# Hybrid encoder layer: pieces multiplied in halves of 256 columns, tokens and sums 16 bytes up in their tiles

## The chip, the cores and the metric

The kernel runs on one core of one Trainium2 chip. The metric is device time in microseconds (us) of one execution, as the median of several runs of the same program. One further execution is taken with the hardware profiler; the profile and the trace below are of that one.

## The reference

One layer of an encoder on 256 tokens of width 4096, all in float32: a layer norm, one wide input projection, a gated short convolution and a windowed attention side by side, one output projection, a residual and a second layer norm.

```python
h = layer_norm(x, emb_ln_g, emb_ln_b)                 # (256, 4096)
p = h @ w_in                                          # (4096, 13312): c_b c_c c_h c_z | q k v | z
y_conv = c_b * centred_short_conv(c_c * c_h, conv_w) * silu(c_z)
y_attn = banded_window_attention(a_q, a_k, a_v, sink) * silu(a_z)
y = concatenate([y_conv, y_attn]) @ w_out             # (4096, 4096)
out = layer_norm(2 ** 0.25 * h + y, ln_g, ln_b)
```

Nearly all arithmetic is in the two projections.

## The kernel before

**Numbers in two halves.** TensorE multiplies in a reduced float32 (F32R). To keep the accuracy, each operand is split in a high half, which is the rounded number, and a low half, which is what the rounding left. A product is then three matmuls: high by high, high by low, low by high. ScalarE writes the high half of the weights (`split_hi`, L203) and VectorE the low half (`split_lo`, L207).

**Operands.** The tokens are the stationary operand: tile `xT` (L228) holds, turned, 32 blocks of 128 rows, each with 256 tokens high and 256 tokens low. The weights stream through as the moving operand. They come from HBM over SyncE's queue in units that a fixed list of steps names (`steps`, L116), into raw tiles (`load`, L139; `loads`, L159), and the halves go to the tiles `whi` and `wlo`, three of each, 8192 bytes a partition.

**Two kinds of steps.** A *piece* is four blocks of 128 rows by 512 columns of weights. `mm` (L237) multiplies it for the input projection and `mm_out` (L904) for the output projection: per block and per half of the tokens three matmuls of 512 columns into a PSUM bank. A *pair* is a Strassen-like step: two blocks of rows by two halves of 256 columns, seven products instead of eight. VectorE adds up sums of the weights' blocks (`sums`, L169), sums of the tokens lie in the tiles `SC`, `SC2` and, in the output projection, `SCy` (`x_sums`, L638; `y_sums`, L997), and `mm_pair` (L257) does 7 × 3 matmuls of 256 columns into the accumulators `acc` and `pacc`. Most column chunks of the input projection have 18 blocks in pieces and 14 in pairs; five chunks of the output projection have four pairs. The last two chunks of the output projection are 256 columns wide, so their matmuls in `mm_out` have 256 columns already.

**Placement.** Tiles of a pool lie one behind the other in each partition. `xT` is 65,536 bytes and the weights' pool follows it at once, so pieces have tokens and weights that both start at multiples of 128 bytes. For pairs the split writes the seven blocks 16 elements, that is 64 bytes, lower in the tile (`SHIFT`, L51; `dst`, L192), and `split_lo` then cuts `wh` and `wl` to these seven blocks, so that `mm_pair` reads block `w - 1`. `SC`, `SC2` and `SCy` start at multiples of 128 bytes too.

**Order.** Every engine takes its instructions in the order in which the program lists them. In the loop over the input steps (L802) step j comes as: the matmuls of j, the high half of step j + 3, work due at j (ends of chunks, attention, convolution), new loads, the weight sums of j + 4, the low half of j + 3. The loop over the output chunks (L1007) has the same order. So the halves run three steps ahead of the matmuls, and there are three tiles for each half.

Of the kernel before, what the change touches and what calls it, by code (L numbers as in the profile page):

```python
# [8 lines left out]
F32 = mybir.dt.float32  # L9
F32R = mybir.dt.float32r  # L10
AF = mybir.ActivationFunctionType
ALU = mybir.AluOpType
AX = mybir.AxisListType

P = 128
D = 4096
S = 256
KT = D // P
# [14 lines left out]
W = 512  # L33
PK = PIECE // W
# [6 lines left out]
HW = W // 2  # L41
HT = S // 2
NP = 7
# [4 lines left out]
OP = 4  # L48
OUT_ORDERS = ["s" * 8] * 2 + ["sSsSsSsSss"] * 5 + ["", ""]
N_W = 3  # L50
SHIFT = 16  # L51


def units(ci):
# [32 lines left out]
def npairs(ci):  # L87
    return PAIRS[ci] if ci < OUT else OUT_ORDERS[ci - OUT].count("S")
# [11 lines left out]
def encoder_kernel(ctx: ExitStack, tc: tile.TileContext, x, emb_g, emb_b, wi, ws, conv_w, sink, wo, ln_g, ln_b, out):  # L100
    nc = tc.nc
    PSUM = bass.MemoryType.PSUM

    const = ctx.enter_context(tc.tile_pool(name="const", bufs=1))
    wpool = ctx.enter_context(tc.tile_pool(name="wpool", bufs=3))
    small = ctx.enter_context(tc.tile_pool(name="small", bufs=4))
# [13 lines left out]
    is_pair = lambda j: steps[j][0] in ("pair", "opair")  # L120

    raw, wh, wl = {}, {}, {}
    psc = pw = pc = R = None
# [62 lines left out]
    def part(j, t):  # L186

        if len(raw[j].shape) == 3:
            return t if len(t.shape) == 3 else t.rearrange("p (i n) -> p i n", i=2)
        return t[:, HW:] if is_pair(j) else t[:, 0:4 * HW] if steps[j][0] == "half" else t  # L190

    def dst(j, t):  # L192

        return t[:, HW - SHIFT:8 * HW - SHIFT] if is_pair(j) and len(raw[j].shape) == 2 else part(j, t)

    def half_tile(j, name):
        if j < len(steps) - 1:
            return wpool.tile([P, PIECE], F32R, name=name)
        (_, k), bs = w_bufs(j)
        user[bs[k]] = j  # L200
        return bs[k][0].tile([P, PIECE], F32R, name=bs[k][1], bufs=1)

    def split_hi(j):  # L203
        wh[j] = half_tile(j, "whi")
        nc.scalar.activation(dst(j, wh[j]), part(j, raw[j]), AF.Copy)  # L205

    def split_lo(j):  # L207
        wl[j] = half_tile(j, "wlo")
        nc.vector.tensor_tensor(dst(j, wl[j]), part(j, raw[j]), dst(j, wh[j]).bitcast(F32), op=ALU.subtract)  # L209
        if is_pair(j):  # L210
            c0 = HW if len(raw[j].shape) == 3 else HW - SHIFT
            wh[j], wl[j] = wh[j][:, c0:c0 + 7 * HW], wl[j][:, c0:c0 + 7 * HW]
        raw.pop(j)

    def split(j):
        if j < len(steps):
            split_hi(j)
            split_lo(j)
# [6 lines left out]
    cw = const.tile([P, CONV_T, 3], F32, name="cw")  # L225
    sk = const.tile([P, HEADS], F32, name="sk")

    xT = const.tile([P, KT, 2 * S], F32R, name="xT")  # L228
    musd = small.tile([P, 2, 4], F32, name="musd", bufs=1)
    eps_t = small.tile([P, 1], F32, name="eps_t", bufs=1)  # L230
    nc.vector.memset(eps_t, LN_EPS)
    small.tile([P, 40], F32, name="gap", bufs=1)


    acc = {}
# [1 line left out]
    def mm(j):  # L237
        _, ci, q = steps[j]
        hi, lo = wh.pop(j), wl.pop(j)
        first = j == 0 or steps[j - 1][1] != ci  # L240
        last = j == N_IN - 1 or steps[j + 1][1] != ci
        pk, k0 = (2, 2 * q) if steps[j][0] == "half" else (PK, q * PK)
        for k in range(pk):
            kt = k0 + k
            for i in range(2):
                if first and k == 0:
                    acc[ci, i] = ps_acc.tile([P, W], F32, name="acc")
                a = acc[ci, i]
                xh, xl = xT[:, kt, i * P:(i + 1) * P], xT[:, kt, S + i * P:S + (i + 1) * P]
                hk, lk = hi[:, k * W:(k + 1) * W], lo[:, k * W:(k + 1) * W]  # L250
                nc.tensor.matmul(a, xh, hk, start=(first and k == 0), stop=False)  # L251
                nc.tensor.matmul(a, xh, lk, start=False, stop=False)  # L252
                nc.tensor.matmul(a, xl, hk, start=False, stop=(last and k == PK - 1))  # L253

    pacc, SC = {}, None

    def mm_pair(j):  # L257


        _, ci, p = steps[j]  # L260
        hi, lo = (t.pop(j).rearrange("p (b w) -> p b w", w=HW) for t in (wh, wl))
        last = p == npairs(ci) - 1
        if p == 0:
            for k in range(2):
                pacc[ci, k] = ps_p.tile([P, 2, HW], F32, name="pacc")
        a, b = 2 * p, 2 * p + 1
        x = lambda kt, i: (xT[:, kt, i * HT:(i + 1) * HT], xT[:, kt, (2 + i) * HT:(3 + i) * HT])
        sc = lambda n: (SC[p][:, 0, n, :], SC[p][:, 1, n, :])
        p0, p1, c0, c1 = pacc[ci, 0], pacc[ci, 1], acc[ci, 0], acc[ci, 1]
        for (ah, al), w, o, opens, closes in (  # L270
                (x(a, 0), 2, p0[:, 0, :], True, False), (x(b, 0), 3, c0[:, 0:HW], False, False),
                (sc(2), 1, c0[:, HW:W], False, False), (x(b, 1), 7, c1[:, 0:HW], False, False),
                (sc(0), 5, p1[:, 1, :], True, False), (x(a, 1) if ci < OUT else sc(3), 6, p0[:, 1, :], False, True),
                (sc(1), 4, p1[:, 0, :], False, True)):
            nc.tensor.matmul(o, ah, hi[:, w - 1, :], start=(opens and p == 0), stop=False)  # L275
            nc.tensor.matmul(o, ah, lo[:, w - 1, :], start=False, stop=False)  # L276
            nc.tensor.matmul(o, al, hi[:, w - 1, :], start=False, stop=(closes and last))  # L277


    def small_chain(i, dst):  # L280
# [10 lines left out]
    with tc.tile_pool(name="pro", bufs=1) as pro:  # L291
# [15 lines left out]
        first = [wpool.tile([P, PIECE], F32, name=f"first{j}", tag="whi") for j in range(2)]  # L307
# [103 lines left out]
        transp2(2, (1,))  # L411
        turned1(1, 0, t1[0])
        split_hi(2)
        first_mm(0, 1)
        transp2(3, (1,))
        turned1(1, 1, t1[1])
        first_mm(1, 1)
        turned2(2)
        split_lo(2)
        load(5)  # L420
        x_split(2)
# [3 lines left out]
        load(6)  # L425
        transp2(4)
        mm(2)
        turned2(4)
        x_split(4)
        split(4)  # L430
        load(7)
        transp2(5)
        mm(3)
        turned2(5)
        x_split(5)
        split(5)
        load(8)
        transp2(6)
        mm(4)
        turned2(6)  # L440
        x_split(6)
# [17 lines left out]

    ph, phs = ExitStack(), ExitStack()  # L460
    psc = ctx.enter_context(tc.tile_pool(name="psc", bufs=1))
    sc_tiles = [psc.tile([P, n, 2, 3, HT], F32R, name=name) for n, name in ((NP - 2, "SC"), (2, "SC2"))]
    SC = [sc_tiles[p // (NP - 2)][:, p % (NP - 2), :, :, :] for p in range(NP)]
    pw = phs.enter_context(tc.tile_pool(name="pw", bufs=1))
    extra.append((pw, "w6"))
# [336 lines left out]
    for j in range(n_pro, N_IN):  # L802
        kind, ci, q = steps[j]
        if j == z0 + 4:
            extra.clear()
        if j == z0 + 12:
            extra.insert(0, (pw, "w6"))
        mm_pair(j) if kind == "pair" else mm(j)
        split_hi(j + 3)
        for fn, a in later.pop(j, []):  # L810
            fn(*a)
        if kind == "pair" and q == PAIRS[ci] - 1:
            pair_copy(ci)
# [12 lines left out]
        split_lo(j + 3)  # L826
# [77 lines left out]
    def mm_out(j, n, halves, k0=0, k1=None):  # L904
        c0, w, pk, j0 = chunks[n]
        ci, q = steps[j][1:]
        hi, lo = wh[j], wl[j]
        for k in range(k0, k1 or pk):
            s = q * pk + k
            first, last = j == j0 and k == 0, s == KT - 1  # L910
            for i in halves:
                if first:
                    acc[ci, i] = ps_acc.tile([P, 512], F32, name="acc")[:, 0:w]
                o = acc[ci, i]
                yh, yl = xT[:, s, i * P:(i + 1) * P], xT[:, s, S + i * P:S + (i + 1) * P]
                hk, lk = hi[:, k * w:(k + 1) * w], lo[:, k * w:(k + 1) * w]
                nc.tensor.matmul(o, yh, hk, start=first, stop=False)  # L917
                nc.tensor.matmul(o, yh, lk, start=False, stop=False)  # L918
                nc.tensor.matmul(o, yl, hk, start=False, stop=last)  # L919

    def plus_res(n):

# [84 lines left out]
    for n, (c0, w, pk, j0) in enumerate(chunks):  # L1007
        us = out_units(n)
        np_ = sum(u[0] == "opair" for u in us)
        for t, (kind, _, q) in enumerate(us):  # L1010
            j = j0 + t
            if kind == "opair":
                mm_pair(j)
            else:
                mm_out(j, n, (0,) if n == ncs - 1 else (0, 1))
# [114 lines left out]
```

## Time and profile before

| | |
|---|---|
| median of 3 runs | 1528.76 us (1528.3 to 1529.1) |
| profiled execution, whole | 1529.49 us |
| profiled execution, span from first to last instruction | 1527.8 us |
| TensorE clock granted | 1.000 on the mean |
| DMA | 315.65 MB, 207 GB/s on the mean |
| ScalarE, GpSimd busy | 51%, 0% |

Engines in the profile: PE is TensorE's matmul, PEld its weight load (it overlaps PE), DVE is VectorE, ACT ScalarE, POOL GpSimd, SP SyncE. A group's row names line, engine, operation, tiles (out<-in) and shapes, then the count, the busy time in us and the mean duration of one in ns, then the idle time before it and what ended that. A matmul's duration contains the drain of the pipe, which overlaps with the next matmul; the distance between two starts is read from the timeline, whose rows give start in us, duration in us, engine, line, operation, tiles, shape and count.

### The profile page before, as it was taken

The numbers are of one execution on the slowest core, as the hardware profiler recorded it, in microseconds if no ns is written. First come the engines' busy times: TensorE is split into PE (matmuls) and PEld (weight loads), VectorE is DVE, ScalarE is ACT, GpSimd is POOL, SyncE is SP. The second block draws the span as 40 slices with busy tenths as digits, with TensorE's granted clock in tenths as the row PEclk, the third lists the DMA queues.
The fourth block names the chain that finished last, engine by engine and source line by source line (L and its number), as shares of the span: only waits on it lengthen the run. The fifth ranks groups of instructions, "written<-read, shape, count | busy, mean of one in ns | idle before, by whom it ended". The sixth has DMA issues, their size and how long they took to land.

```text
span 1527.8 us, 21818 instructions
## 1 busy us (share of the span) xinstructions
PE 1511.7 (99%) x8879; PEld 1330.0 (87%) x8879; DVE 1329.4 (87%) x1555; ACT 780.7 (51%) x669; POOL 1.3 (0%) x7
## 2 busy tenths in 40 slices
PE   7999999999999999999999999999999999999998
PEld 4888989898988989989889888888988888888897
DVE  7769899999899898998898899989898688888876
ACT  5545546657565655545555455544556444444431
POOL 0000000000000000000000000000000000000000
PEclk9999999999999999999999999999999999999999
DMA  7555654555654556656555655556557655666573
GB/s 289 208 179 193 207 207 162 205 179 196 210 182 171 185 185 205 230 183 234 199 190 202 215 189 202 207 175 234 198 203 291 257 200 215 257 213 214 215 248 131
DMA packets 71716, 315.65 MB, mean 207 GB/s; under 512 B 8544, under 2 KB 12608, under 8 KB 50880
## 3 DMA queue, kind: packets, MB, share of 16 engines
q1 hardware_dynamic: 70608, 312.43, 58.4%
q10 hardware_dynamic: 1008, 1.84, 0.3%
q8 instruction: 69, 1.13, 0.3%
q14 instruction: 31, 0.25, 0.0%
HBM read 305.23 MB, written 8.91 MB: 206 GB/s over the span
## 4 chain that ended last, share of the span: by engine, by line
PE 83%; DVE 12%; ACT 2%; DMA 1%; issue 1%; SPq 0%; ACTq 0%; DVEq 0%
PE acc L252 13%; PE acc L253 13%; PE acc L251 13%; DVE wlo L209 7%; PE acc L918 6%; PE acc L919 6%; PE acc L917 6%; PE pacc L275 4%; PE pacc L277 4%; PE pacc L276 4%; PE acc L275 3%; PE acc L277 3%; PE acc L276 3%; ACT whi L205 2%; DVE w L182 1%
## 5 line engine op out<-in xcount | busy, mean ns | idle before, releaser
L205 ACT ACTIVATE whi<-w 128x2048 fp32r<-128x2048 f32 (+1 forms) x354 | 621.5, 1756 | 621.8 <-DVE w L184 218.2
L209 DVE TENSOR_TENSOR wlo<-w,whi 128x2048 fp32r<-128x2048 f32 (+1 forms) x354 | 736.4, 2083 | 123.7 <-ACT whi L205 123.5
L251 PE MATMUL acc<-whi,xT 128*128 128x512 f32 x988 | 387.4, 392 | 0.0
L252 PE MATMUL acc<-wlo,xT 128*128 128x512 f32 x988 | 386.0, 391 | 0.3
L253 PE MATMUL acc<-whi,xT 128*128 128x512 f32 x988 | 385.1, 390 | 0.0
L252 PEld LDWEIGHTS acc<-wlo,xT 128*128 128x128 f32 x988 | 185.5, 188 | 39.4 <-DVE wlo L209 3.6
L253 PEld LDWEIGHTS acc<-whi,xT 128*128 128x128 f32 x988 | 185.4, 188 | 38.1
L251 PEld LDWEIGHTS acc<-whi,xT 128*128 128x128 f32 x988 | 185.5, 188 | 35.0
L918 PE MATMUL acc<-wlo,xT 128*128 128x512 f32 (+1 forms) x480 | 175.1, 365 | 1.0 <-DVE wlo L209 1.0
L917 PE MATMUL acc<-whi,xT 128*128 128x512 f32 (+1 forms) x480 | 175.1, 365 | 0.0
L919 PE MATMUL acc<-whi,xT 128*128 128x512 f32 (+1 forms) x480 | 174.9, 364 | 0.0
L182 DVE TENSOR_TENSOR w<-w 128x512 f32<-128x512 f32 x179 | 122.3, 683 | 10.2 <-DMA w<-in_ws 10.2
L918 PEld LDWEIGHTS acc<-wlo,xT 128*128 128x128 f32 x480 | 90.6, 189 | 15.3 <-DVE wlo L209 1.7
L275 PE MATMUL acc<-whi,xT 128*128 128x256 f32 x370 | 103.7, 280 | 0.0
L276 PE MATMUL acc<-wlo,xT 128*128 128x256 f32 x370 | 103.7, 280 | 0.0
L277 PE MATMUL acc<-whi,xT 128*128 128x256 f32 x370 | 103.7, 280 | 0.0
L919 PEld LDWEIGHTS acc<-whi,xT 128*128 128x128 f32 x480 | 90.5, 189 | 14.3
L917 PEld LDWEIGHTS acc<-whi,xT 128*128 128x128 f32 x480 | 90.6, 189 | 13.9 <-issue 0.4
L275 PE MATMUL pacc<-whi,xT 128*128 128x256 f32 x350 | 99.8, 285 | 0.0
L276 PE MATMUL pacc<-wlo,xT 128*128 128x256 f32 x350 | 98.3, 281 | 0.0
L277 PE MATMUL pacc<-whi,xT 128*128 128x256 f32 x350 | 98.1, 280 | 0.0
L277 PE MATMUL pacc<-whi,SC 128*128 128x256 f32 x330 | 92.5, 280 | 0.0
(230 smaller groups left out, 2059.4 us busy)
## 6 DMA issues: line engine op xcount, KB each, us to landing
w<-in_wi SPq DMA_DIRECT2D x112, 1024.0 KB
w<-in_ws SPq DMA_DIRECT2D x202, 512.0 KB
w<-in_wo SPq DMA_DIRECT2D x41, 1024.0 KB
R<-in_wo SPq DMA_DIRECT2D x13, 1024.0 KB
x<-in_x SPq DMA_DIRECT2D x7, 512.0 KB
yl<-yd SPq DMA_DIRECT2D x7, 512.0 KB
xc<-in_x SPq DMA_DIRECT2D x14, 256.0 KB
R<-in_ws SPq DMA_DIRECT2D x6, 512.0 KB
```

The source lines that it names most:

```text
L182: nc.vector.tensor_tensor(s01, b22, b12.to_broadcast([P, 2, HW]), op=ALU.add)
L205: nc.scalar.activation(dst(j, wh[j]), part(j, raw[j]), AF.Copy)
L209: nc.vector.tensor_tensor(dst(j, wl[j]), part(j, raw[j]), dst(j, wh[j]).bitcast(F32), op=ALU.subtract)
L251: nc.tensor.matmul(a, xh, hk, start=(first and k == 0), stop=False)
L252: nc.tensor.matmul(a, xh, lk, start=False, stop=False)
L253: nc.tensor.matmul(a, xl, hk, start=False, stop=(last and k == PK - 1))
L275: nc.tensor.matmul(o, ah, hi[:, w - 1, :], start=(opens and p == 0), stop=False)
L276: nc.tensor.matmul(o, ah, lo[:, w - 1, :], start=False, stop=False)
L277: nc.tensor.matmul(o, al, hi[:, w - 1, :], start=False, stop=(closes and last))
L917: nc.tensor.matmul(o, yh, hk, start=first, stop=False)
L918: nc.tensor.matmul(o, yh, lk, start=False, stop=False)
L919: nc.tensor.matmul(o, yl, hk, start=False, stop=last)
```

## The change

Three edits. In `mm` and `mm_out` a matmul of 512 columns becomes two of 256, the three products of the left half first, then those of the right half; stationary operands are named again for each half. The shift of the pairs' weights by 64 bytes goes (`SHIFT`, `dst` and the cut in `split_lo`), so that all weights' blocks start at multiples of 1024 bytes in their tiles. And a new function `shifted` gives tiles that are 32 bytes longer than their content, which begins 16 bytes in: `xT`, `SC` and `SC2` come from it, `SCy` does not. `musd`, `eps_t` and a filler go from the pool `small` to `const`, which, with the 32 bytes of `xT`, moves the weights' pool up by 128 bytes; a second filler makes `small` 128 bytes smaller, so that the pools behind it begin where they began. With that, the tokens and sums start 16 bytes past a multiple of 128 and the weights on one, that is 112 bytes past the tokens modulo 128.

```diff
-SHIFT = 16
+OFF = 4
...
-    def dst(j, t):
-
-        return t[:, HW - SHIFT:8 * HW - SHIFT] if is_pair(j) and len(raw[j].shape) == 2 else part(j, t)
...
-        nc.scalar.activation(dst(j, wh[j]), part(j, raw[j]), AF.Copy)
+        nc.scalar.activation(part(j, wh[j]), part(j, raw[j]), AF.Copy)
...
-        nc.vector.tensor_tensor(dst(j, wl[j]), part(j, raw[j]), dst(j, wh[j]).bitcast(F32), op=ALU.subtract)
-        if is_pair(j):
-            c0 = HW if len(raw[j].shape) == 3 else HW - SHIFT
-            wh[j], wl[j] = wh[j][:, c0:c0 + 7 * HW], wl[j][:, c0:c0 + 7 * HW]
+        nc.vector.tensor_tensor(part(j, wl[j]), part(j, raw[j]), part(j, wh[j]).bitcast(F32), op=ALU.subtract)
...
-    xT = const.tile([P, KT, 2 * S], F32R, name="xT")
-    musd = small.tile([P, 2, 4], F32, name="musd", bufs=1)
-    eps_t = small.tile([P, 1], F32, name="eps_t", bufs=1)
+    def shifted(pool, shape, name, **kw):
+
+        n = math.prod(shape)
+        t = pool.tile([P, n + 2 * OFF], F32R, name=name, **kw)[:, OFF:OFF + n]
+        names = "abcd"[:len(shape)]
+        return t.rearrange(f"p ({' '.join(names)}) -> p {' '.join(names)}", **dict(zip(names[1:], shape[1:])))
+
+    xT = shifted(const, (KT, 2 * S), "xT")
+    musd = const.tile([P, 2, 4], F32, name="musd")
+    eps_t = const.tile([P, 1], F32, name="eps_t")
     nc.vector.memset(eps_t, LN_EPS)
-    small.tile([P, 40], F32, name="gap", bufs=1)
+    const.tile([P, 8], F32, name="gap")
+    small.tile([P, 24], F32, name="gap2", bufs=1)
...
-                hk, lk = hi[:, k * W:(k + 1) * W], lo[:, k * W:(k + 1) * W]
-                nc.tensor.matmul(a, xh, hk, start=(first and k == 0), stop=False)
-                nc.tensor.matmul(a, xh, lk, start=False, stop=False)
-                nc.tensor.matmul(a, xl, hk, start=False, stop=(last and k == PK - 1))
+                for c in range(0, W, HW):
+                    o, sl = a[:, c:c + HW], slice(k * W + c, k * W + c + HW)
+                    nc.tensor.matmul(o, xh, hi[:, sl], start=(first and k == 0 and c == 0), stop=False)
+                    nc.tensor.matmul(o, xh, lo[:, sl], start=False, stop=False)
+                    nc.tensor.matmul(o, xl, hi[:, sl], start=False, stop=(last and k == PK - 1 and c > 0))
...
-            nc.tensor.matmul(o, ah, hi[:, w - 1, :], start=(opens and p == 0), stop=False)
+            nc.tensor.matmul(o, ah, hi[:, w, :], start=(opens and p == 0), stop=False)
...
-    sc_tiles = [psc.tile([P, n, 2, 3, HT], F32R, name=name) for n, name in ((NP - 2, "SC"), (2, "SC2"))]
+    sc_tiles = [shifted(psc, (n, 2, 3, HT), name) for n, name in ((NP - 2, "SC"), (2, "SC2"))]
...
-                hk, lk = hi[:, k * w:(k + 1) * w], lo[:, k * w:(k + 1) * w]
-                nc.tensor.matmul(o, yh, hk, start=first, stop=False)
-                nc.tensor.matmul(o, yh, lk, start=False, stop=False)
-                nc.tensor.matmul(o, yl, hk, start=False, stop=last)
+                for c in range(0, w, HW):
+                    oc, sl = o[:, c:c + HW], slice(k * w + c, k * w + c + HW)
+                    nc.tensor.matmul(oc, yh, hi[:, sl], start=(first and c == 0), stop=False)
+                    nc.tensor.matmul(oc, yh, lo[:, sl], start=False, stop=False)
+                    nc.tensor.matmul(oc, yl, hi[:, sl], start=False, stop=(last and c + HW == w))
```

The two other matmuls of `mm_pair` change in the same way as the first.

More of the change, by code (lines that the diff above doesn't have):

```diff
@@ L274, in mm_pair @@
                 (sc(1), 4, p1[:, 0, :], False, True)):
-            nc.tensor.matmul(o, ah, hi[:, w - 1, :], start=(opens and p == 0), stop=False)
-            nc.tensor.matmul(o, ah, lo[:, w - 1, :], start=False, stop=False)
-            nc.tensor.matmul(o, al, hi[:, w - 1, :], start=False, stop=(closes and last))
+            nc.tensor.matmul(o, ah, hi[:, w, :], start=(opens and p == 0), stop=False)
+            nc.tensor.matmul(o, ah, lo[:, w, :], start=False, stop=False)
+            nc.tensor.matmul(o, al, hi[:, w, :], start=False, stop=(closes and last))
     def small_chain(i, dst):
```

## The prediction

> **What bounds the kernel now.** I read the page's busy table and its chain first, then the instruction groups with shapes kept apart, then single starts in the timeline.
>
> ```profile
> span 1527.8 us, 21818 instructions
> ...
> PE 1511.7 (99%) x8879; PEld 1330.0 (87%) x8879; DVE 1329.4 (87%) x1555; ACT 780.7 (51%) x669; POOL 1.3 (0%) x7
> ...
> PE 83%; DVE 12%; ACT 2%; DMA 1%; issue 1%; SPq 0%; ACTq 0%; DVEq 0%
> ```
>
> TensorE (PE) is busy 99% of the span and is 83% of the chain that ended last, with VectorE (DVE) second. So the time is nearly the number of matmuls times the distance from one start to the next. The counts, by form:
>
> ```profile
> L251 PE MATMUL acc<-whi,xT 128*128 128x512 f32 x988 | 387.4, 392 | 0.0
> L917 PE MATMUL acc<-whi,xT 128*128 128x512 f32 x368 | 143.3, 389 | 0.0
> L275 PE MATMUL acc<-whi,xT 128*128 128x256 f32 x370 | 103.7, 280 | 0.0
> L275 PE MATMUL pacc<-whi,xT 128*128 128x256 f32 x350 | 99.8, 285 | 0.0
> L275 PE MATMUL pacc<-whi,SC 128*128 128x256 f32 x330 | 92.4, 280 | 0.0
> L275 PE MATMUL acc<-whi,SC 128*128 128x256 f32 x165 | 46.2, 280 | 0.0
> L917 PE MATMUL acc<-whi,xT 128*128 128x256 f32 x112 | 31.9, 285 | 0.0
> L275 PE MATMUL pacc<-whi,SCy 128*128 128x256 f32 x60 | 16.9, 281 | 0.0
> L275 PE MATMUL acc<-whi,SCy 128*128 128x256 f32 x20 | 5.6, 281 | 0.0
> L917 PE MATMUL acc<-w,xT 128*128 128x256 f32 x16 | 4.6, 290 | 0.0
> ```
>
> Each row stands for three lines (high·high, high·low, low·high). So pieces have 3 × (988 + 368) = 4068 matmuls of 512 columns, pairs 3 × 1295 = 3885 of 256, of which 3 × 80 = 240 read SCy, and the two narrow output chunks 3 × 128 = 384 of 256. The mean durations contain the drain of the pipe, so the pace is read from starts:
>
> ```profile
> 23.50 3.60 PE L378 MATMUL acc<-first,hT 128*128 128x512 f32 x8
> 26.93 0.60 PE L361 MATMUL att<-ident,x 128*128 128x128 f32 x4
> ...
> 230.16 0.28 PE L277 MATMUL acc<-whi,xT 128*128 128x256 f32 x1
> ...
> 231.86 0.28 PE L277 MATMUL pacc<-whi,SC 128*128 128x256 f32 x1
> ...
> 660.28 0.28 PE L275 MATMUL pacc<-whi,xT 128*128 128x256 f32 x1
> ...
> 665.23 0.39 PE L251 MATMUL acc<-whi,xT 128*128 128x512 f32 x1
> ...
> 667.95 0.28 PE L275 MATMUL pacc<-whi,xT 128*128 128x256 f32 x1
> ...
> 1489.77 0.28 PE L917 MATMUL acc<-whi,xT 128*128 128x256 f32 x1
> ...
> 1498.65 0.28 PE L919 MATMUL acc<-whi,xT 128*128 128x256 f32 x1
> ...
> 1514.96 3.29 PE L1066 MATMUL pacc<-ident 128*128 128x128 f32 x28
> 1518.10 0.31 PE L959 MATMUL att<-ident,t 128*96 128x128 f32 x1
> ```
>
> Pieces: 12 starts from 665.23 to 667.95, 226.7 ns each. Pairs: 42 from 660.28 to 665.23, 117.8 ns. The narrow chunks: 74 from 1489.77 to 1498.65, 120.0 ns. Some pairs run otherwise: 15 from 230.16 to 231.86, 113.3 ns, the same instructions on the same kind of tiles.
>
> Between 512 and 256 columns at one placement lie 226.7 - 120.0 = 106.7 ns. That is what 256 columns cost, and what is over is an extra **per matmul**: 13.3 ns for pieces and narrow chunks, 11.1 for pairs, 6.6 in the faster pairs. The three fit the placement: in pieces and narrow chunks moving weights and stationary tokens both start at multiples of 128 bytes, in pairs the weights lie 64 bytes below one. The plain float32 matmuls at the ends take twice as long for a column: the early ones 3.43/8 = 428.8 ns for 512, which at half the pace above are 4 × 106.7 = 426.7, an extra of 2.1. The ones on the identity, 128 columns, take 3.14/28 = 112.1 ns, an extra of 5.4 over 106.7, and each has a weight load of its own. So the 13.3 is no fixed charge of a matmul: it depends on where and how fast two streams of reads run beside each other. I infer that the moving stream and the next weight load delay each other; no row shows this itself.
>
> **The change, part by part.** *Two halves for each piece.* 4068 matmuls of 226.7 ns become 8136 of x ns, where x is the distance that 256 columns take at the new placement, weights 112 bytes past the tokens modulo 128. Loads double with them. That their number is bearable is shown by the pairs, where each 256 columns already have a load. *The new placement* also moves 3885 - 240 = 3645 pair matmuls and the 384 narrow ones to x. For the pairs' pace so far:
>
> ```profile
> L276 PE MATMUL acc<-wlo,xT x370: 276/281/281, 128.3 to 1454.9; 128*128 128x256 f32 x185
> ```
>
> The row, from the answer on line 276, gives minimum, median and maximum duration. The 281 goes with 117.8 ns between starts and the 276 with 113.3; counted over all starts, about one in eight is of the fast sort, so the mean is 117.8 - 4.5/8 = 117.2. SCy is not moved, so its 240 matmuls have weights and sums both on multiples of 128, as the narrow chunks do now: 240 × (120.0 - 117.8) = +0.5 us.
>
> *A wait that comes sooner.* The second matmul of a piece needs the low half, and it now stands behind 107 ns less work:
>
> ```profile
>   PEld acc L252: 3.6, 12
>   PEld acc L918: 1.7, 2
> ```
>
> These rows tell who waited for the subtraction on line 209. At 14 waits the cover shrinks by 0.107 us, +1.5 us in all. *The splits without the shift* write at multiples of 128 instead of 64 below:
>
> ```profile
> L209 DVE TENSOR_TENSOR wlo<-w,whi 128x1792 fp32r<-128x1792 f32 x179 | 360.9, 2020 | 40.5 <-ACT whi L205 40.5
> L209 DVE TENSOR_TENSOR wlo<-w,whi 128x2048 fp32r<-128x2048 f32 x152 | 347.6, 2287 | 80.5 <-ACT whi L205 80.3
> ```
>
> Shifted and unshifted cost 1.13 and 1.12 ns a column, so nothing. The small tiles that change pools, the fillers, and the 32 bytes by which later pools move are no instruction: 0. No DMA is added or moved, and no queue is passed.
>
> **The sum** on TensorE is 4068 × (2x - 226.7) + 3645 × (x - 117.2) + 384 × (x - 120.0) + 2000 ns, which is 12,165 × x - 1393.5 us. It is zero at x = 114.6 ns, and each nanosecond is 12.2 us.
>
> What is x? No row has this placement. Below stands 106.7 + 2.1 = 108.8, the smallest extra of any row; above stands 120.0, the largest of the steady 256-column rows. By distance in bytes the nearest is the 120.0; by extra it can't be told, since three placements would be needed to draw a line and there are two. I take 110.5, about midway between the two float32 rows (108.8 and 112.1), whose streams run with a load and hardly collide. The reason is that the same pair instructions drop from 117.8 to 113.3 in stretches without any change of address, so the meeting of the streams can be avoided in part by phase alone. It is a choice between far ends and is weighed as such below. It gives 12,165 × 110.5 - 1393.5 = -49 us.
>
> What is late next is VectorE:
>
> ```profile
> 155.00:600.00 445.00, 404.76 (x501) 1.00 0.56 189
> 600.00:1168.00 568.00, 516.07 (x564) 1.00 0.60 208
> ...
> 756.40:799.30 42.90, 42.83 (x263) 38.12 (x263) 40.94 (x48) 22.39 (x17) 0.00 (x0) 1.00 0.57 197
> ```
>
> In the windows (length, then VectorE's busy time; in the third row PE, PEld, DVE) it is busy 920.8 of the 1013 us from 155 to 1168, 91%, and 40.94 of 42.9 in the chunk at 756.4. TensorE would need 3.3% less, 41.5 us there, so such chunks have next to nothing to spare, and only three halves of weights are kept ahead. I charge a quarter of the two thirds that fall in this stretch: +8 us. Forecast: 1529.5 (the profiled execution: span 1527.8 and 1.7 around it) - 49 + 8 = 1488.5, less the 0.7 by which the median of the runs is below that execution: **1488 us**. Its own range goes from 1462 (x = 109, VectorE takes nothing) to 1502 (x = 112.1, VectorE takes 3).
>
> The Trainium skill, "TensorE: Matmul & The Clock Gate", section "Wait — 56ns, not 53.3ns?", gives a fixed cost of about 2.5 ns per matmul over the streaming time; by it halving the pieces would cost 4068 × 2.5 = +10 us and give nothing back. The float32 row with 2.1 agrees, the 13.3 of the pieces does not. "SBUF — State Buffer", section "Who interferes with whom", says TensorE's two read ports are independent; by it placement could matter nothing. The 120.0 beside 117.8 and 113.3 speaks against that, though they belong to different tiles.
>
> **The rivals.**
> 1. *Slower: the extra is paid per matmul wherever the tiles lie.* Place: the pieces, where the number of matmuls doubles. For it: every 256-column row in steady flow has 11.1 or 13.3, and 512 columns pay it no more than 256 do. Against it: the 113.3 stretches. It decides from x = 114.6 on. At the pairs' 117.8 it costs 12,165 × 117.8 - 1393.5 = +39.5, 1568 us. At 120.0, the nearest row in bytes, it costs +66, 1594 us. The skill's fixed cost per matmul is this case, only with a smaller price.
> 2. *The fast state of the pairs becomes the rule everywhere,* x = 113.3. Two halves then take exactly one old piece (226.6), and only pairs and narrow chunks gain: -15, 1513 us.
> 3. *VectorE takes the gain over* in 155 to 1168 us, as its 91% allows: a third of the 49 is left, 1512 us.
>
> **How the numbers follow.** The forecast 0.46, rival 1 at 117.8 0.20 and at 120.0 0.14, rival 2 0.11, rival 3 0.04; the rest, x close to the 114.6, 0.05. About 0.2% (3 us) is what a measurement can tell from no change. Faster: 0.46 + 0.11 + 0.04 = 0.61; within: 0.05; slower: 0.34. A range from 1462 to 1570 leaves out rival 1's upper price and a little at the low end, under 0.2.
>
> **What would show it.** In the changed kernel the piece lines should appear twice as often at 128x256, and a mean duration of about 273 or 274 ns would mean x = 110.5, since the drain adds 163 (276 - 113.3, 281 - 117.8). A 276 there is rival 2, 281 or 283 rival 1. SCy's rows should stand at 283, above those of SC: if they equal SC's, placement is not what counts. VectorE's busy time should stay at 1329 us, its share reach 89% or more, and waits of TensorE on line 209 grow from the few above; if they grow to tens of microseconds, rival 3 holds. The forecast fails above all if x, which no row shows, isn't under 112.

## The result and the profile after

| | before | changed |
|---|---|---|
| median | 1528.76 us (5 runs, 1528.12 to 1529.1) | 1579.65 us (5 runs, 1575.05 to 1580.26) |
| profiled execution, whole | 1529.49 us | 1580.26 us |
| ratio | | 1.0328, 95% interval 1.0316 to 1.0339 |

The change makes the kernel 3.3% slower, 51 us. It lies above the predicted range (1462 to 1570) and on the other side of the forecast.

The page of the changed kernel, busy table and chain of waits:

```profile
span 1578.5 us, 29953 instructions
...
PE 1564.9 (99%) x12947; PEld 1549.1 (98%) x12947; DVE 1331.6 (84%) x1555; ACT 780.0 (49%) x669; POOL 1.3 (0%) x7
...
PE 98%; DVE 1%; DMA 0%; ACT 0%; issue 0%; SPq 0%; ACTq 0%
```

The chain was 83% TensorE and 12% VectorE; now nearly nothing but TensorE is left in it. VectorE does the same work in more time, so its share fell from 87% to 84%. Weight loads rose by the 4068 added matmuls and now fill 98% of the span.

The instruction groups of the changed kernel, shapes kept apart (L253 to L255 are `mm`, L277 to L279 `mm_pair`):

```profile
L253 PE MATMUL acc<-whi,xT 128*128 128x256 f32 x1976 | 562.7, 285 | 0.0
L254 PE MATMUL acc<-wlo,xT 128*128 128x256 f32 x1976 | 560.5, 284 | 0.0
...
L278 PE MATMUL acc<-wlo,xT 128*128 128x256 f32 x370 | 104.8, 283 | 0.0
...
L278 PE MATMUL pacc<-wlo,SC 128*128 128x256 f32 x330 | 93.7, 284 | 0.0
...
L278 PE MATMUL pacc<-wlo,SCy 128*128 128x256 f32 x60 | 16.9, 282 | 0.0
```

Pieces come twice as often (1976 for 988) with a mean duration of 284, not 273 or 274; less the 163 to 164 of the drain that is a distance of about 120 ns. Pairs on SC went from 280 to 284 with no change in their number or shape. The starts say it directly, in the timeline of TensorE:

```profile
665.02 0.28 PE L277 MATMUL pacc<-whi,SC 128*128 128x256 f32 x1
665.15 0.28 PE L278 MATMUL pacc<-wlo,SC 128*128 128x256 f32 x1
665.26 0.28 PE L279 MATMUL pacc<-whi,SC 128*128 128x256 f32 x1
665.39 0.28 PE L277 MATMUL pacc<-whi,xT 128*128 128x256 f32 x1
...
1220.42 0.28 PE L921 MATMUL acc<-wlo,xT 128*128 128x256 f32 x1
...
1558.16 0.28 PE L922 MATMUL acc<-whi,xT 128*128 128x256 f32 x1
```

From the fifth to the last row stand 2819 starts without a gap: 337.74 us / 2818 = 119.85 ns. The first four show what lies behind that mean: the distances alternate, about 119 and 121 in the trace's nanoseconds. In other places four distances repeat (120, 115, 121 and 117 or 118), 118.5 on the mean. The windows of the changed kernel (length, then PE, PEld, DVE, ACT, POOL busy, the granted clock, the share of DMA, GB/s) show that nothing else came to the front:

```profile
155.00:600.00 445.00, 445.00 (x3744) 444.99 (x3743) 393.98 (x487) 259.95 (x279) 0.00 (x0) 1.00 0.55 186
600.00:1168.00 568.00, 567.86 (x4739) 567.62 (x4738) 500.05 (x552) 277.74 (x188) 0.00 (x0) 1.00 0.57 196
```

TensorE has not a gap left, at a granted clock of 1.00, and VectorE is down to 894.0 of 1013 us.

Adding up the distances from each start to the next over all matmuls of a kind in the two traces tells where the 51 us are. *Long distances* are those over 260 ns for 512 columns and over 160 for 256, counted with what they have above one matmul in steady flow; they are in the pieces' sum. The trace puts 5.3 us of them down to VectorE's low half before (the 3.6 and 1.7 us of the prediction's rows on line 209) and none after; most of the rest stands at the first use of a low half or right behind a wait, and the trace names no one for it.

| us | pieces | of them long distances | pairs | attention's matmuls | narrow chunks |
|---|---|---|---|---|---|
| before | 931.5 | 7.3 | 456.9 | 26.7 | 46.5 |
| changed | 976.3 | 2.5 | 466.1 | 23.7 | 46.4 |
| difference | +44.8 | -4.8 | +9.2 | -3.0 | -0.1 |

### The profile page after: what moved, and what is told of

Its sections match the earlier page's. It is cut to its first block, busy times and chain, and to the rows that moved or that the text cites. A ratio compares the mean times of both kernels' runs of the same rounds, so it can differ in the third digit from the quotient of the medians.

```text
span 1578.5 us, 29953 instructions
## 1 busy us (share of the span) xinstructions
PE 1564.9 (99%) x12947; PEld 1549.1 (98%) x12947; DVE 1331.6 (84%) x1555; ACT 780.0 (49%) x669; POOL 1.3 (0%) x7
## 4 chain that ended last, share of the span: by engine, by line
PE 98%; DVE 1%; DMA 0%; ACT 0%; issue 0%; SPq 0%; ACTq 0%
PE acc L254 15%; PE acc L253 15%; PE acc L255 15%; PE acc L920 7%; PE acc L921 7%; PE acc L922 7%; PE pacc L278 6%; PE pacc L279 6%; PE pacc L277 6%; PE acc L277 4%; PE acc L279 4%; PE acc L278 4%; PE att L492 1%; DVE st L330 0%; PE att L603 0%; PE acc L380 0%
## 5 line engine op out<-in xcount | busy, mean ns | idle before, releaser
L253 PE MATMUL acc<-whi,xT 128*128 128x256 f32 x1976 | 562.7, 285 | 0.0
L254 PE MATMUL acc<-wlo,xT 128*128 128x256 f32 x1976 | 560.5, 284 | 0.0
L255 PE MATMUL acc<-whi,xT 128*128 128x256 f32 x1976 | 560.5, 284 | 0.0
L254 PEld LDWEIGHTS acc<-wlo,xT 128*128 128x128 f32 x1976 | 374.8, 190 | 0.1
L253 PEld LDWEIGHTS acc<-whi,xT 128*128 128x128 f32 x1976 | 374.9, 190 | 0.0
L255 PEld LDWEIGHTS acc<-whi,xT 128*128 128x128 f32 x1976 | 374.8, 190 | 0.0
L920 PE MATMUL acc<-whi,xT 128*128 128x256 f32 x848 | 241.4, 285 | 0.0
L922 PE MATMUL acc<-whi,xT 128*128 128x256 f32 x848 | 241.2, 284 | 0.0
L921 PE MATMUL acc<-wlo,xT 128*128 128x256 f32 x848 | 241.2, 284 | 0.0
L920 PEld LDWEIGHTS acc<-whi,xT 128*128 128x128 f32 x848 | 161.1, 190 | 0.4 <-issue 0.4
L921 PEld LDWEIGHTS acc<-wlo,xT 128*128 128x128 f32 x848 | 161.1, 190 | 0.0
L922 PEld LDWEIGHTS acc<-whi,xT 128*128 128x128 f32 x848 | 161.0, 190 | 0.0
L277 PE MATMUL acc<-whi,xT 128*128 128x256 f32 x370 | 105.0, 284 | 0.0
L279 PE MATMUL acc<-whi,xT 128*128 128x256 f32 x370 | 105.0, 284 | 0.0
L278 PE MATMUL acc<-wlo,xT 128*128 128x256 f32 x370 | 104.8, 283 | 0.0
L277 PE MATMUL pacc<-whi,xT 128*128 128x256 f32 x350 | 100.9, 288 | 0.0
L279 PE MATMUL pacc<-whi,xT 128*128 128x256 f32 x350 | 99.3, 284 | 0.0
L278 PE MATMUL pacc<-wlo,SC 128*128 128x256 f32 x330 | 93.7, 284 | 0.0
```

The costliest lines, as they stand in the source:

```text
L253: nc.tensor.matmul(o, xh, hi[:, sl], start=(first and k == 0 and c == 0), stop=False)
L254: nc.tensor.matmul(o, xh, lo[:, sl], start=False, stop=False)
L255: nc.tensor.matmul(o, xl, hi[:, sl], start=False, stop=(last and k == PK - 1 and c > 0))
L277: nc.tensor.matmul(o, ah, hi[:, w, :], start=(opens and p == 0), stop=False)
L278: nc.tensor.matmul(o, ah, lo[:, w, :], start=False, stop=False)
L279: nc.tensor.matmul(o, al, hi[:, w, :], start=False, stop=(closes and last))
```

## The experiments

Two explanations stood from the start. Either 256 columns always pay an extra near 13 ns, however operands lie (the prediction's first rival); or the distance depends on placement, and this placement is a bad one. "rel" below is the start of the weights less that of the tokens, modulo 128 bytes: 0 in the pieces before, 64 in the pairs before, 112 in the changed kernel. Distances are means of starts in steady flow, unless a row is shown. The kernel before ran at 1528.5 to 1529.7 us beside each experiment.

### One half of the change each

**e1**: the kernel before with the halves in `mm` and `mm_out`, as in the change's last hunks, and nothing moved.

> The kernel before with the pieces in halves of 256 columns and nothing else: tokens and weights of pieces stay on multiples of 128 bytes, pairs keep their 64 bytes. Theory A (each matmul pays an extra of about 13 ns whatever its width, so doubling their number costs it once more): pieces go at 120.0 ns a start, +54 us on TensorE, of which the waits for VectorE that vanish give some 10 back: about 1574 us. Theory B (the new placement is what costs): halves at the old place cost little, 1525 to 1540 us.

1564.28 us, ratio 1.0227 (1.0212 to 1.0242).

**e2**: the changed kernel with `mm` and `mm_out` of before, 512 columns each.

> The changed kernel with pieces of 512 columns again: the placement alone. Theory A: pieces stay at 226 to 227 ns a start, pairs go from 117.2 to 119.7 as in the changed kernel, 3645 of them, +9 us: about 1538 us. Theory B: pieces at the new place need clearly more than 227 ns each, and the time is over 1555 us.

1550.79 us, ratio 1.0136 (1.0119 to 1.0153). Groups of e1 and then of e2, shapes kept apart:

```profile
L253 PE MATMUL acc<-wlo,xT 128*128 128x256 f32 x1976 | 560.2, 284 | 0.0
...
L277 PE MATMUL acc<-wlo,xT 128*128 128x256 f32 x370 | 102.2, 276 | 0.0
```

```profile
L253 PE MATMUL acc<-wlo,xT 128*128 128x512 f32 x988 | 390.8, 396 | 0.0
...
L277 PE MATMUL acc<-wlo,xT 128*128 128x256 f32 x370 | 104.3, 282 | 0.0
```

Both parts are losses, and both times lie between those of theories A and B. Halves alone cost 34.6 us: each pays 120.0, the pace of the narrow chunks, so two take 240 instead of 226.7. In the sums of starts the pieces rise by 48.2 and the pairs fall by 11.7, since 178 of 185 pairs now run at 113.4 (276 in the second row), against 30 before, and not one byte of their operands was moved. The new placement alone costs 21.1 us: 512 columns go from 226.7 to 231 to 238 ns (mean duration 396, before 391), pairs to 118.6 (282). So halving is bad with either placement and the placement is bad for whole pieces too.

### Which distance from the tokens is good?

**e3 and e4**: the kernel before, with another shift for each of the seven pairs of a chunk, so that one run measures seven places.

```diff
-SHIFT = 16
+SHIFTS = [4, 8, 12, 16, 20, 24, 28]      # e4: [1, 2, 3, 0, 32, 64, 128]
...
+        sh = SHIFTS[steps[j][2]] if is_pair(j) else 0
```

> The kernel before with another place for each pair of a chunk: pair p has its weights 16 (p + 1) bytes below the multiple of 128, so 112, 96, 80, 64, 48, 32 and 16 bytes past the tokens. Theory A: all seven stand between 117 and 120.5 ns a start, and the time is within 5 us of before. Theory B: some place stands 5 ns or more apart from the others, 112 above all of them.

> As the scan before, with the pairs' weights 4, 8, 12, 0, 128, 256 and 512 bytes below the multiple of 1024. Theory A: 0, 128, 256 and 512 are alike at 120, as the narrow chunks are, and the shifts inside 16 bytes stand between 117 and 121 ns. Theory B: the shifts inside 16 bytes stand apart by 5 ns or more.

1530.68 and 1534.89 us, one run each.

| weights down by, bytes | 4 | 8 | 12 | 16 | 32 | 48 | 64 | 80 | 96 | 112 | 0, 256, 512 | 128 |
|---|---|---|---|---|---|---|---|---|---|---|---|---|
| ns, pairs | 117.4 | 120.0 | 121.7 | 117.2 | 118.1 | 118.5 | 117.8 | 119.35 | 118.3 | 115.6 | 120.0 | 118.8 |

Four bytes are worth up to 4.5 ns (12 beside 16), with no order in it. Places equal modulo 128 don't all agree (128 beside 0). Each place belongs to one position of a pair in its chunk here, so what stands in front differs too. In the output projection, where every pair follows a whole piece, the places still differ: 117.2, 120.1, 121.8 and 120.0 for 4, 8, 12 and 0 bytes (5 pairs each, e4). The 115.6 is a mean of two paces: 14 pairs at 113.4, 9 near 118.9; e16 takes that up.

**e5 and e6**: the pieces read their weights 0, 16, ... 112 bytes up, by the step's number modulo 8; e5 in 512 columns, e6 in halves. The last block of a piece is left out, since the read would go past the tile, and the block before it is multiplied a second time. The edit of e5 in `mm` (`mm_out` has the same):

```diff
+SCAN = [0, 4, 8, 12, 16, 20, 24, 28]
...
+                s_, kk = (SCAN[j % 8], min(k, PK - 2)) if steps[j][0] == "in" else (0, k)
-                hk, lk = hi[:, k * W:(k + 1) * W], lo[:, k * W:(k + 1) * W]
+                hk, lk = hi[:, kk * W + s_:(kk + 1) * W + s_], lo[:, kk * W + s_:(kk + 1) * W + s_]
```

> The kernel before, with pieces of 512 columns read 0, 16, 32, 48, 64, 80, 96 and 112 bytes up in their tiles, by the step's number modulo 8 (the products of each piece's last block are replaced by a second use of the block before it). Theory A2 (every matmul pays about 13 ns, and the place moves this by a few ns either way): 0 is 226.7 ns a start, the others 222 to 236, each some ns apart. Theory B2 (112 bytes is a bad place for itself and the others are like 0): seven at 226 to 228 and 112 at 233.

> The same scan with the pieces in halves of 256 columns. Theory A2: all eight places between 113.3 and 121 ns a start, so that halves win nowhere against 226.7 for both; the 64 of the pairs at 113.3 to 117.8. Theory C (there is a place where the extra goes): one place under 112 ns.

1537.91 and 1553.06 us, one run each.

| weights up by (rel) | 0 | 16 | 32 | 48 | 64 | 80 | 96 | 112 |
|---|---|---|---|---|---|---|---|---|
| 512 columns, ns | 226.6 | 231.65 | 233.3 | 233.1 | 228.9 | 231.1 | 233.4 | 230.95 |
| 256 columns, ns | 120.0 | 117.6 | 116.7 | 118.3 | 117.3 | 119.15 | 120.0 | 113.3 |

For 512 columns the place of before is the best of eight; for 256 it is the worst, together with 96, and 112 the best. From the timeline of e6, the first and last of 48 starts of a piece at 112:

```profile
108.99 0.28 PE L254 MATMUL acc<-whi,xT 128*128 128x256 f32 x1
...
114.31 0.28 PE L256 MATMUL acc<-whi,xT 128*128 128x256 f32 x1
```

5.32 us / 47 = 113.2 ns. After the first twelve distances, in which it settles, all 665 others of the pieces at this place are 113 or 114 ns, 113.3 on the mean. Here rel is 112, as in the changed kernel, and even the distance in bytes from the start of `xT` is the same, 65,648. Only, tokens start at 0 and weights at 112, and not 16 and 0 modulo 128. The changed kernel runs at 119.7. The distance between tokens and weights, then, isn't what decides by itself. The steps ahead lie at other places in e6; e12 takes that away.

### Is it the amount that is loaded?

**e7**: in `mm` of the kernel before, the third product takes 64 tokens instead of 128, except in the last block of a chunk.

```diff
+                z = P if last and k == PK - 1 else P // 2
-                nc.tensor.matmul(a, xl, hk, start=False, stop=(last and k == PK - 1))
+                nc.tensor.matmul(a[0:z, :], xl[:, 0:z], hk, start=False, stop=(last and k == PK - 1))
```

> The kernel before, where the third product of the input projection's pieces (low tokens by high weights) uses 64 of the 128 tokens, so its weight load has half the columns (the output lacks these parts). The load of the third product goes beside the second product's stream. Theory D (the load and the stream delay each other): the distance from the second product's start to the third's drops from 226.7 by about half of the 13.3, to 218 to 222 ns, and the other two distances stay. Theory E (a fixed charge for each matmul, whatever is loaded): all three stay at 226 to 227 ns.

1530.47 us, one run. Weight loads of e7, grouped with shapes kept apart:

```profile
L252 PEld LDWEIGHTS acc<-whi,xT 128*128 128x128 f32 x988 | 185.5, 188 | 81.4
L254 PEld LDWEIGHTS acc<-whi,xT 128*64 128x64 f32 x936 | 125.7, 134 | 38.6
```

The load got shorter, 134 for 188 ns, but the pace didn't: the three lines stand at 230.4, 229.0 and 230.5 ns from their start to the next, before at 226.7 on all three. Less to load made every third matmul different, and the fixed pace was lost (224 to 236). That the load and the stream hold each other up in proportion to what is loaded falls.

### The same distance, the other way round

**e9, e10, e11, e12** put tokens and sums at multiples of 128 again and move the weights. In e9 and e11 the halves lie 112 bytes up, in e10 at 0, with the high halves in tiles 8320 bytes apart and the low ones in one block, 8192 apart; e9 and e10 multiply in halves, e11 in 512 columns. Of the edit, the weights' tiles:

```diff
-            return wpool.tile([P, PIECE], F32R, name=name)
+            if name == "whi":
+                return wpool.tile([P, PIECE + 32], F32R, name=name)[:, OFF:OFF + PIECE]
+            if not low:
+                low.extend([wpool.tile([P, 3 * PIECE + 32], F32R, name=name, bufs=1), 0])
+            k, low[1] = low[1], (low[1] + 1) % 3
+            return low[0][:, OFF + k * PIECE:OFF + (k + 1) * PIECE]
```

> The changed kernel, in which tokens and sums go back to multiples of 128 bytes and all weights' halves move 112 bytes up instead: the same distance in bytes, at other places (the tiles of weights have room for it, the small tiles of the attention have fewer buffers). Theory H (both places count, not the distance alone; weights at 112 and tokens at 0 ran at 113.3 in the scan): pieces in halves 113.3, no dearer than 226.7 for both before, pairs 113.3 to 114: some 15 us off, 1512 to 1518 us. Theory I (the distance alone counts, the scan was favoured by the steps ahead): 119 to 120 ns everywhere, 1575 to 1582 us like the changed kernel.

> The same kernel with weights, tokens and sums all on multiples of 128 bytes. Theory H: 120.0 ns a start for pieces and pairs: 8136 x 120.0 against 4068 x 226.7 is +54 us, 3645 x 2.8 for the pairs +10, less some 5 of waits that vanish: about 1587 us. Theory I says the same, so this run gives the price of the place itself: its difference from the run with 112.

> Weights 112 bytes up, tokens and sums on multiples of 128, pieces of 512 columns. By the scan of 512 columns (231 at this place): 4068 x 4.3 = +17 us for pieces; pairs at 113.3 to 117, between -2 and -15: 1531 to 1546 us, so that here halves win against whole pieces. Rival: 226.7 as at every multiple of 128, then 1514 to 1530 us.

1558.52 us (ratio 1.0196, 1.0182 to 1.021), 1560.8 and 1537.04 us (one run each). The 113.3 of e6 didn't come: 117.7 in e9, without a fixed pace (113 to 124). In e10, with every start at 0, the 120.0 that this place has with the old tiles didn't come either, but 118.1. In e11 113 of 158 pieces run at 227 ns and 42 near 237, and the time lies in the range of its first expectation. For TensorE the tiles differ from those of e6 above all in that high and low halves are no longer a multiple of 1024 bytes apart. **e12** puts that right: all six halves in one block, 8192 bytes apart, 112 up, and every step at this one place. That needs the third piece's high half to be split somewhat later at the beginning.

```diff
+        if not big:
+            big.append(wpool.tile([P, 6 * PIECE + 32], F32R, name="whl", bufs=1))
+        k += 3 * (name == "wlo")
+        return big[0][:, OFF + k * PIECE:OFF + (k + 1) * PIECE]
```

> The changed kernel with tokens and sums on multiples of 128 bytes and all six halves' tiles in one block, 112 bytes up, so that high and low halves lie multiples of 8192 bytes apart (one split of the prologue comes a little later). Theory J (a fixed pace of 113.3 needs tokens on 128 and the halves alike in their places): pieces 113.3, pairs 113.3, 1512 to 1520 us. Theory K (the scan's 113.3 came from the steps ahead at other places, and a kernel with one place for all finds no such pace): 117 to 120 ns and 1555 to 1582 us.

1531.87 us, ratio 1.002 (1.0011 to 1.0029). The first start of a piece and the last of 1947 in e12's timeline, then its page:

```profile
1188.06 0.28 PE L924 MATMUL acc<-whl,xT 128*128 128x256 f32 x1
...
1408.66 0.28 PE L923 MATMUL acc<-whl,xT 128*128 128x256 f32 x1
```

```profile
PE 77%; DVE 17%; ACT 3%; issue 2%; DMA 1%; SPq 0%; ACTq 0%; DVEq 0%
...
L256 PE MATMUL acc<-whl,xT 128*128 128x256 f32 x1976 | 548.4, 278 | 3.9 <-DVE whl L215 3.4
```

220.60 us / 1946 = 113.36 ns, pieces and pairs alike. The matmuls are those of the changed kernel, as many and in the same order; where their operands lie is worth 48 us. It still isn't faster than before: two times 113.3 is 226.7, one old piece; the pairs gain 13.0 us and the narrow chunks 2.0. That goes to long distances in the pieces (17.1 us for 7.3), to the later start (+4.3 us) and to the attention's matmuls (+1.8). Of the 17.1 us the trace puts 9.3 down to VectorE's low half, for 5.3 before, and the chain is 17% DVE; 2.5 lie between 36 and 40 us, where the granted clock is 0.50 and one start follows the other after 213 ns.

**e13** was to give pieces 512 columns at 0 and pairs 112 up.

> The kernel before, whole pieces of 512 columns on multiples of 128, the six halves' tiles in one block, and only the pairs' weights 112 bytes up instead of 64 down. Theory J: a pair needs some ten matmuls to fall into 113.3, so the mean is about 115.5 against 117.2 before: 5 to 8 us off, 1521 to 1525 us. Theory K: pairs 117 to 118, no change within 3 us.

2233.82 us, ratio 1.4609 (1.4589 to 1.4629). It tells nothing of places: raised by 112 bytes, the last block of a pair reached into the tile of the next step, which overwrote it, and the steps waited for each other (ScalarE's splits alone 808.5 us for the matmuls of line 256, by the trace's list of waits). With tiles that hold it, this placement was not tried for all pairs; e3's pair 16 bytes down lies at the same place modulo 128 and ran at 117.2 behind pieces of 512 columns.

### What the entry does

In e1 the pairs ran faster without being moved. What changed for them is the matmuls in front. **e8** halves only the last block of a piece that stands ahead of a pair (twelve matmuls of 256 columns), **e14** only the second half of the tokens in it (six), **e15** only its very last matmul (two).

```diff
-                nc.tensor.matmul(a, xl, hk, start=False, stop=(last and k == PK - 1))
+                cut = is_pair(min(j + 1, len(steps) - 1)) and k == PK - 1 and i == 1
+                for c in range(0, W, HW) if cut else ():
+                    nc.tensor.matmul(a[:, c:c + HW], xl, hk[:, c:c + HW], start=False, stop=(last and c > 0))
+                if not cut:
+                    nc.tensor.matmul(a, xl, hk, start=False, stop=(last and k == PK - 1))
```

That is e15; `mm_out` is cut in the same way.

> The kernel before, where only the last block of a piece that stands ahead of a pair is multiplied in halves of 256 columns. In the halves-only kernel 178 of 185 pairs ran at 113.4 ns a start, against 30 of 185 before. Theory F (the phase in which a pair is entered sets its pace): most pairs go at 113.4, 3645 or more matmuls by up to 4 ns, less 6 matmuls of 13 ns for each such piece (some 90), so 6 to 9 us off: about 1521 us. Theory G (the long stretch of 256-column matmuls ahead did it): pairs stay at 117.0, and the time is 5 to 8 us above before.

> The kernel before, in which only the last block of the second half of the tokens of a piece ahead of a pair is multiplied in halves: six matmuls of 256 columns lead into a stretch of pairs instead of twelve (e8). They add 92 x 3 matmuls at 13.3 ns = +3.7 us. Theory P, a stretch keeps the pace in which it is entered, and any 256-column entry gives the pairs 113.4 ns: pairs -10 us as in e8, 1522 to 1524 us. Rival L, the settling takes some ten matmuls and ends elsewhere after six: pairs stay at 117.8 and the time is 1531 to 1533 us.

> The same with only the very last matmul of such a piece cut in two: +92 x 13.3 ns = +1.2 us. Theory P: pairs at 113.4 ns, -10 us, so 1519 to 1521 us. Rival L: pairs at 117.8 ns, 1529 to 1531 us.

| | median, us | ratio (interval) | pairs at 113.4 | pairs, us | pieces, us | of them long distances |
|---|---|---|---|---|---|---|
| before | | | 30 of 185 | 456.9 | 931.5 | 7.3 |
| e8, twelve | 1529.03 | 1.0002 (0.9993 to 1.0011) | 154 | 447.0 | 939.9 | 8.4 |
| e14, six | 1527.16 | 0.999 (0.9981 to 0.9999) | 158 | 446.7 | 938.4 | 10.4 |
| e15, two | 1524.83 | 0.9975 (0.9966 to 0.9984) | 156 | 446.8 | 937.0 | 11.7 |

From the timeline of e15 (the row with x2 is the matmul cut in two):

```profile
261.99 0.39 PE L251 MATMUL acc<-whi,xT 128*128 128x512 f32 x1
262.21 0.39 PE L252 MATMUL acc<-wlo,xT 128*128 128x512 f32 x1
262.44 0.40 PE L255 MATMUL acc<-whi,xT 128*128 128x256 f32 x2
262.67 0.29 PE L279 MATMUL pacc<-whi,xT 128*128 128x256 f32 x1
...
267.34 0.28 PE L281 MATMUL pacc<-whi,SC 128*128 128x256 f32 x1
```

42 pair matmuls from 262.67 to 267.34: 4.67 us / 41 = 113.9 ns with the settling, on operands that stayed where they were. Two matmuls of 256 columns are entry enough. The three kernels hold a control, too: in each chunk with seven pairs one pair stands behind a piece of only two blocks, where `k == PK - 1` never holds, so nothing is cut. All 23 such pairs stay at 117.8 in e8, e14 and e15, while 154, 158 and 156 of the other 162 run at 113.4; in e1, where these short pieces are halved as well, the 23 run at 113.3.

The pace came as theories F and P said, the time didn't: it lies 3 to 8 us above what they gave. e15 is 0.25% faster than the kernel before, and so faster than both kernels of this document. Of the 10.1 us that its pairs gain, 92 more matmuls take 92 × 13.3 ns = 1.2, and long distances 4.4. For most of these VectorE is named, 8.7 us in 19 waits of e15:

```profile
PEld acc L252 <- DVE wlo L209: 6.4, 16, 0.7
...
PEld acc L922 <- DVE wlo L209: 2.3, 3, 1.1
```

It was 5.3 us in 14 waits before.

**e16** moves the weights of all pairs to the place of e3's last pair (SHIFT = 28), **e17** adds e14's lead of six.

> The kernel before with the pairs' weights 112 bytes down instead of 64, for all pairs, so that weights start 16 bytes past the tokens modulo 128. In e3 this place gave 113.4 ns in 14 of 23 pairs and 118.9 in the other 9, always at the last pair of a chunk. Theory of place: about the same share for all pairs, mean 115.5, 3645 x (115.5 - 117.2) = -6 us, 1522 to 1524 us. Rival, the share came from the position of that pair in its chunk (how it is entered) and not from the place: pairs at 117.8 to 118.9 in most, 1529 to 1535 us.

> e14 and e16 together. If place and entry act independently and both help, pairs at 113.4 ns throughout: -13.5 + 3.7 us, 1518 to 1520 us. If the entry alone counts: as e14. If the new place has its own entry and the lead gives it the wrong one: pairs at 118.9, 1537 to 1540 us.

e16: 1528.71 us, ratio 0.9999 (0.9991 to 1.0008). e17: 1534.0 us, ratio 1.0034 (1.0022 to 1.0046). The same group in e16 and in e17:

```profile
L276 PE MATMUL pacc<-wlo,SC 128*128 128x256 f32 x330 | 92.1, 279 | 0.0
```

```profile
L283 PE MATMUL pacc<-wlo,SC 128*128 128x256 f32 x330 | 92.7, 281 | 0.0
```

In e16 158 of 185 pairs run at 116.7 and 27 near 118.9; the 113.4 of e3 isn't there, so it didn't come from the place alone, and neither expectation held. In e17 it is the reverse, 157 near 118.9 and 28 at 116.7. The lead that helps at one place (117.8 to 113.4) hurts at the other (116.7 to 118.9), which was the third case foreseen for e17, with a smaller loss. In e17 the 23 pairs behind the short pieces, which are not cut, are among the 28 that stay at 116.7. So each of these two places has a few paces of its own, and the entry picks one of them.

## Why the prediction was wrong

**The step that failed is the choice of x = 110.5.** By it two halves would take 5.7 ns less than an old piece (2 × 110.5 - 226.7); the runs show x = 119.7 at this placement (long distances aside), so they take 12.7 ns more. The sum over x was sound. At 119.7 it gives 12,165 × 119.7 - 1393.5 = +62.7 us, and +51 came. Its terms against the sums of starts: pairs 3645 × (119.7 - 117.2) = +9.1, measured +9.2; pieces 4068 × (239.4 - 226.7) = +51.7, measured +44.8. Of those 6.9 us, 4.8 are long distances that are no longer there and 2.1 the stretches of 228 to 236 ns in which old pieces settled; further 3.0 left the attention's matmuls, and the +2.0 for earlier waits and SCy didn't come. In the changed kernel no matmul of the pieces waits for VectorE.

**How x was chosen.** The prediction bounded it by 108.8, from plain float32 matmuls, and 120.0, and went to the middle of the float32 rows, because the pairs drop from 117.8 to 113.3 without a change of address. No run showed reduced-float32 matmuls of 256 columns with steady starts under 113.3, over all the places tried. The float32 rows were no neighbours: 256 columns take twice as long there, and the extra of 2.1 carries over to nothing here. The nearest row in bytes, which the prediction named and didn't take (120.0), would have been right within 0.3 ns, but by luck: the same 112 bytes with tokens at 0 give 113.3 in e6 and e12. The inference that the stream and the next load delay each other was shown by no run; e7 speaks against the simple form of it, in which less load means less delay.

**"The 113.3 can be reached by phase alone"** was right, and e15 lives on it; that x could fall below it was not. At 113.3, the second rival, two halves only equal one old piece, so halving has nothing to win in the pieces at any pace that was seen.

**The rivals.** The first, near its upper price of 120.0, is what came about in the time. Its wording (the extra is paid wherever the tiles lie) is too strong, for e12 pays half of it. Its bounds were 1568 and 1594; 1579.65 lies between, and the 0.14 on the upper price was too low. The second rival's pace came in e12, by another placement, at 1531.87 and not 1513: the pairs gained 13.0 us of the 14.2 that it gives them (3645 × 3.9 ns), and long distances, about half of them waits for VectorE, and the later start took it back. The third, VectorE, shows there and in e15, never in the changed kernel, where TensorE is the slower one. The charge of +8 us for it had no occasion.

**The signs to look for.** 284 as a mean duration was named as the sign of the first rival (281 or 283), and was it. "SCy's rows should stand at 283, above those of SC" failed: 282 beside 284 for SC. By the prediction's own words that speaks against placement, but in a pair SCy's matmuls stand between those on `xT`, and since a stretch has one pace, a row can't show what its own operands alone would do. It was no test. Shift and no shift in the splits cost the same, as said: 360.9 us before for the 179 subtractions of pairs and 360.9 after (2020 ns each), in the groups of both.

The Trainium skill, "TensorE: Matmul & The Clock Gate", section "Wait — 56ns, not 53.3ns?", gives a fixed 2.5 ns per matmul; by it e1 would have cost an estimated 4068 × 2.5 ns = +10 us. It measured +34.6, and over the 106.7 of the columns the runs show 6.6 (e12) and 13.3 ns (e1), so the measurement decides. The Trainium skill, "SBUF — State Buffer", section "Who interferes with whom", holds TensorE's two read ports for independent; by it the placement should do nothing. The changed kernel and e12 differ in it by 48 us. No run shows whether the ports are what collides.

**What stays open** is why there are such paces: 113.3, 120.0 and 226.7 are multiples of 6.67 ns, and others are cycles (353.3 for three, 119 and 121 in turn). This was seen and not explained.

## What to carry to other kernels

Where an engine's time is count times pace, a change that doubles the count stands or falls with a pace at the new shape, so measure that pace in one run with several placements at once, as e6 did, before summing with a guess from another kind of instruction. A pace belongs to a whole stream: places of all operands, the spacing of the tiles, and the matmul that leads in; a good offset can't be carried over as a distance. And before making the busiest engine faster look how much the second leaves over: in e15 4.4 us of the 10.1 gained went to long distances, most of them waits for VectorE.

## What the runs showed of the hardware that was not expected

- Reduced-float32 matmuls with a weight load each settle into fixed paces: 113.3 or 120.0 ns for 256 columns and 226.7 for 512, at a granted clock of 1.00, within some twelve matmuls (e6: all 665 distances at 113 or 114 thereafter). Other places give cycles (117.8 in the pairs before) or none (113 to 124, e9).
- Starts four bytes apart change it: 117.4, 120.0 and 121.7 ns at 4, 8 and 12 bytes (e4). So does the spacing of the tiles: 113.4 with high and low halves 8192 bytes apart (e12), 117.7 with the high halves 8320 apart (e9).
- The same instructions on the same addresses run at 113.4 or 117.8, according to what leads in: 156 of 185 pairs at 113.4 where two matmuls of 256 columns lead into the pairs (e15), 30 where whole pieces do (before). At another place such a lead, of six, does the opposite (e17).
- Halving what a load carries (188 to 134 ns) doesn't quicken the stream (e7: 229 to 230.5 ns, before 226.7).
